# A two-layer decoder trunk on one core: the value pass with the coefficients standing in the array instead of the value rows

## The chip, the core and the metric

The kernel runs on one core of a Trainium2 chip. TensorE (PE) multiplies, VectorE (DVE), ScalarE (ACT) and GpSimd (POOL) do element work, SyncE (SP) issues most of the DMAs. A matrix product here has a stationary operand, which is loaded into the array (at most 128 columns), and a moving operand, which streams past it (at most 512 columns); the result is summed in a bank of PSUM, 128 partitions by 512 floats. There are eight banks. The metric is the device time of one execution in microseconds (us).

## The reference

Each of two layers mixes the 256 tokens (layer 0 an mLSTM, layer 1 an RG-LRU, both with cross-attention to a fixed memory), normalises, and then applies PEER, a mixture of 16,384 experts of which each token uses 8 x 16. The change is in the last two lines of PEER:

```python
u = u_tab[eid]
act = gelu(einsum('nhkd,nd->nhk', u, xb))
coef = (gw * act)
y = einsum('nhk,nhkd->nd', coef, v_tab[eid])
...
x = layer_norm(DN_ALPHA * x + y, ln2_g[i], ln2_b[i])
```

`v_tab` holds 16,384 rows of 1,024 floats. The kernel computes `y` for most tokens as a dense product over all experts, with a coefficient of zero where a token does not use one.

## The kernel before

**Tokens.** Of the 256 tokens the first N = 192 go the dense way. The last NS = 64 go row by row: `few` gathers each token's rows of `u` and `v` by indirect DMAs from POOL's queue (L1104) and sums them on DVE (L1124 for `u`, L1128 for `v`), 128 partitions by 1,024 elements an operation, 128 operations for `u` and 128 for `v` in a layer. `deal` (L1131) hands out these operations: each step of a pass adds a rate from RATES to a credit, and at 1.0 one operation is issued. At the step with `i + 2 == CLOSE` whatever is left is issued at once, and a DMA on SP's queue moves half of the sum to the other partitions.

**Values.** The dense coefficients of layer and pass lie in `wglo` and `wghi`: 128 blocks (one per group of 128 experts) of 128 partitions by 192 tokens. The value pass is the loop `for i in range(P)` in `peer_layer`: one step for each of the 128 groups. A step takes the group's 128 x 1,024 value rows from a ring of five raw buffers, filled by SP's DMAs. Since a product of float32 precision is made of three products of a shorter format, the rows are split: ACT casts them to the high part `wH` (L123), DVE subtracts for the low part `wL` (L138), in a ring of HL_BUFS = 3 pairs. The block of coefficients is split in the same way two steps ahead (`coef`: ACT L270, DVE L271) into a tile `cc`: 192 high columns and 192 low ones.

**Products.** In `products` the value rows stand and the coefficients move: for each of eight slices of 128 output columns, `wH` stands while the 384 columns of `cc` stream (L1373), then `wL` stands while the 192 high columns stream (L1374). The result is transposed: 128 output columns by 192 tokens, in eight banks, one for each slice.

**The end of a pass.** The last two groups (`kept`) are held back and multiplied slice by slice at the end, with three products of 192 columns each (L201 to L203). Then, for each slice, a product with the identity folds the high-by-low sums in (L1171), ACT copies the slice out (L1434), PE transposes it back to tokens in two parts (L1416 for tokens 0 to 127, the first tile; L1417 for tokens 128 to 191 of the second tile), and DVE adds it to `x` (L1422) and takes statistics (L1427). After the last slice `norm` forms mean and root for both tiles (L380 to L383), and scales: for part of the first tile ACT and POOL do it (`scale_beside`, L356 to L360), for the rest DVE (L344 and L349). In layer 1 the result is stored; that is the program's end. In layer 0 the rows are transposed for the next layer (`turn`, L370, then ACT L374 and DVE L375), and between these transposes PE works at six pieces of layer 1's memory keys and values (`memory`); then the RG-LRU layer begins with the query product over the new `x`, 24 products for the first four slices of `x` and 24 for the last four.

**Order.** All engines run their instructions in the order in which this code is written; nothing is rescheduled. An instruction waits for what it reads and for the buffers it writes.

## Time and profile before

| | us |
|---|---|
| median of three runs (1654.86 to 1657.91) | 1655.14 |
| the profiled execution | 1655.38 |
| its span, first to last instruction | 1653.6 |
| layer 0: first product of the value pass, first transpose for layer 1, first query product | 540.09, 845.65, 852.93 |
| layer 1: first product of the value pass, last transpose, end of the span | 1340.90, 1641.26, 1653.6 |

In the rows below, an engine's times are from the span's start. PE is one row per product or per run of products; "idle before" is the time in which the engine did nothing, with what ended it. Products are pipelined: the duration of one (0.36 us for 384 columns) is longer than the distance to the next, so the pace of a pass is read from the distance of starts. PEclk is the clock granted to TensorE, 1.00 being 2.4 GHz and 0.50 being 1.2 GHz.

### The profile page before, as it was taken

The page shows a single profiled execution, that of the slowest core. Times are in us where ns is not written, and L with a number is a line of the kernel's source. Part 1 is how long each engine was busy: PE and PEld are TensorE (multiplying, and loading weights), DVE is VectorE, ACT ScalarE, POOL GpSimd, SP SyncE. Part 2 cuts the span into 40 slices and gives each one's busy share as a digit, 9 for nine tenths or more (in the row PEclk, how much of TensorE's full clock was granted, in tenths as well). Part 3 has the DMA queues.
Part 4 walks back from the last instruction along what each step waited for, and adds up shares of the span by engine and source line. Part 5 has one row for each costly group of instructions (what it writes and reads, how often), then busy time and mean ns, then how long its engine had stood idle before and what let it go on. Part 6 is the DMA issues. An engine that isn't in the chain of part 4 may idle for free. (4 is left out here: it accounts for less than half of the span.)

```text
span 1653.6 us, 31410 instructions
## 1 busy us (share of the span) xinstructions
PE 1626.6 (98%) x11693; PEld 1607.6 (97%) x11693; DVE 1405.8 (85%) x2865; ACT 787.2 (48%) x1527; POOL 451.1 (27%) x362
## 2 busy tenths in 40 slices
PE   9999999999999999999999999999999999999996
PEld 9999999999999999999989899999999999999996
DVE  6676787899999898998878958888999988999976
ACT  6564334432226555555658442345222455555554
POOL 3004202432223333332100250133222333343301
PEclk9999999999999999999999999999999999999998
DMA  7655468988889999998856255799888999999973
GB/s 253 210 179 200 154 218 321 355 319 314 319 308 355 329 351 350 348 360 314 289 170 206 101 176 193 279 339 353 309 313 311 340 330 345 355 349 356 349 242 116
DMA packets 133784, 470.54 MB, mean 285 GB/s; under 512 B 14972, under 2 KB 18816, under 8 KB 133376
## 3 DMA queue, kind: packets, MB, share of 16 engines
q1 hardware_dynamic: 94984, 330.89, 57.4%
q0 software_dynamic: 36864, 134.23, 21.6%
q10 hardware_dynamic: 1784, 3.41, 0.6%
q8 instruction: 92, 1.51, 0.3%
q14 instruction: 60, 0.49, 0.1%
HBM read 465.46 MB, written 1.31 MB: 282 GB/s over the span
## 5 line engine op out<-in xcount | busy, mean ns | idle before, releaser
L138 DVE TENSOR_TENSOR wL<-raw,wH 128x1024 fp32r<-128x1024 f32 (+3 forms) x436 | 514.0, 1181 | 177.8 <-ACT wH L123 175.4
L123 ACT CAST wH<-raw 128x1024 fp32r<-128x1024 f32 (+2 forms) x445 | 456.1, 1027 | 390.2 <-PE bank L1373 235.5
L1373 PE MATMUL bank<-cc,wH 128*128 128x384 f32 x2016 | 575.6, 360 | 4.9 <-DVE cc L271 4.9
L1374 PE MATMUL bank<-cc,wL 128*128 128x192 f32 x2016 | 505.5, 251 | 1.9 <-DVE wL L138 1.9
L274 PE MATMUL bank<-xF,raw 128*128 128x192 f32 x2624 | 454.6, 328 | 0.0
L274 PEld LDWEIGHTS bank<-xF,raw 128*128 128x128 f32 x2624 | 423.0, 190 | 0.0
L1374 PEld LDWEIGHTS bank<-cc,wL 128*128 128x128 f32 x2016 | 386.5, 192 | 2.1 <-DVE wL L138 2.1
L1373 PEld LDWEIGHTS bank<-cc,wH 128*128 128x128 f32 x2016 | 379.5, 188 | 5.4 <-DVE cc L271 5.4
L1104 POOL DMA_INDIRECT row<-in_v_dram,lot x128 | 209.0, 1632 | 358.8 <-DVE rep L1128 315.6
L1104 POOL DMA_INDIRECT row<-in_u_rows_dram,lot x128 | 144.9, 1132 | 466.6 <-DVE wghi L1198 187.7
L1161 PE MATMUL bank<-xHL,wH 128*128 128x384 f32 x736 | 217.3, 360 | 0.0
L1162 PE MATMUL bank<-xHL,wL 128*128 128x192 f32 x736 | 184.5, 251 | 0.0
L1128 DVE SCALAR_TENSOR_TENSOR rep<-row,coefs,rep 128x1024 f32<-128x1024 f32 x124 | 158.4, 1278 | 0.1
L1124 DVE CUSTOM_DVE_ANT_0 row<-row,rep 128x1024 f32<-128x1024 f32 x128 | 155.7, 1217 | 0.0
L1162 PEld LDWEIGHTS bank<-xHL,wL 128*128 128x128 f32 x736 | 140.7, 191 | 0.0
L201 PE MATMUL bank<-xHL,wH 128*128 128x256 f32 x488 | 138.4, 284 | 0.0
L1161 PEld LDWEIGHTS bank<-xHL,wH 128*128 128x128 f32 x736 | 138.4, 188 | 0.0
L203 PE MATMUL bank<-xHL,wL 128*128 128x256 f32 x488 | 136.6, 280 | 0.1
L202 PE MATMUL bank<-xHL,wH 128*128 128x256 f32 x488 | 136.3, 279 | 0.0
L1195 ACT ACTIVATE wghi<-bank 128x192 f32<-128x192 f32 (+23 forms) x96 | 24.1, 252 | 206.9 <-PE bank L274 206.9
L202 PEld LDWEIGHTS bank<-xHL,wH 128*128 128x128 f32 x488 | 92.9, 190 | 0.3 <-DVE xHL L462 0.2
L203 PEld LDWEIGHTS bank<-xHL,wL 128*128 128x128 f32 x488 | 92.0, 189 | 0.4 <-DVE wL L138 0.3
(337 smaller groups left out, 1985.7 us busy)
## 6 DMA issues: line engine op xcount, KB each, us to landing
raw<-in_u_dram SPq DMA_DIRECT2D x256, 512.0 KB, 4.9
raw<-in_v_dram SPq DMA_DIRECT2D x256, 512.0 KB, 6.5
raw<-in_w_q_dram SPq DMA_DIRECT2D x32, 512.0 KB, 4.2
raw<-in_w_out_dram SPq DMA_DIRECT2D x16, 512.0 KB, 3.8
raw<-in_w0qx_dram SPq DMA_DIRECT2D x8, 512.0 KB, 5.1
raw<-in_w0v_dram SPq DMA_DIRECT2D x8, 384.0 KB, 5.0
raw<-in_w0o_dram SPq DMA_DIRECT2D x8, 384.0 KB, 2.9
raw<-in_w1x_dram SPq DMA_DIRECT2D x8, 384.0 KB, 3.0
```

The lines of the kernel that those rows point to most:

```text
L123: (nc.vector.tensor_copy if self.cast_dve else nc.scalar.copy)(h[:, c], r[:, c])
L138: rest = lambda l=l, r=r, h=h, c=slice(k, n): nc.vector.tensor_sub(l[:, c], r[:, c], h[:, c].bitcast(F32))
L202: mm(out, sH, mL, start=False, stop=False, skip_group_check=True)
L203: mm(out, sL, mH, start=False, stop=stop, skip_group_check=True)
L274: self.nc.tensor.matmul(out, lhsT, rhs, start=start, stop=stop, skip_group_check=True)
L1104: self.nc.gpsimd.indirect_dma_start(to, None, rows, bass.IndirectOffsetOnAxis(ap=self.lot[:, 0, n:n + 1].bitcast(I32), axis=0))
L1124: nc.vector.tensor_tensor_reduce(r, r, rep, 1.0, 0.0, ALU.mult, ALU.add, sums[:, n:n + 1])
L1128: nc.vector.scalar_tensor_tensor(acc[0] if n == NS - 1 else rep, r, c, rep, op0=ALU.mult, op1=ALU.add)
L1161: mm(two(g[:, :2 * N]), h[:, c], two(self.xHL[:, dt, :])[:, :, :N], start=dt == 0, stop=False, skip_group_check=True)
L1162: mm(g[:, :N], l[:, c], self.xH[:, dt, :N], start=False, stop=False, skip_group_check=True)
L1373: mm(y[s][:, :2 * N], h[:, c], cc[:, :2 * N], start=i_ == 0, stop=False, skip_group_check=True)
L1374: mm(y[s][:, :N], l[:, c], cc[:, :N], start=False, stop=False, skip_group_check=True)
```

## The change

The roles in the value pass are exchanged. Now 128 or 64 columns of coefficients stand, and 512 columns of value rows move. `cc` gets 64 more columns: [192 high | 192 low | the 64 high ones of tokens 128 to 191 again], the last by one more ACT copy. Columns 320 to 447 are then the low and the high coefficients of the 64 tokens of the second tile in one stationary tile, so that one product over `wH` gives low-by-high in partitions 0 to 63 and high-by-high in 64 to 127 (`second`, L1418); the high ones over `wL` (64 columns, L1416) are added to the lower half. The first tile takes three products (`first`, L1427, L1428, L1425). The result has tokens in partitions, as `x` has: four banks, no fold, no copy and no transpose back.

At the end of a pass the last HALVED groups (2 in layer 0, 6 in layer 1) are held back whole and the last KEPT (3 and 7) for half of the first tile. Their order is: the second tile, then the first tile's left half, then its right half in two quarters. For that layer 1 gets four more pairs of value buffers and seven more `cc` tiles, in the space of `wglo`, which is free from step 64 on, and looks further ahead from step 107 on (`lead`). `norm` has a new branch: ACT copies the upper half of the second tile's banks out, DVE adds both halves to `x`, and the second tile's statistics, root and scaling come between those of the first tile's quarters; POOL has no part in it. The dealing is spread: rate 0.55 to step 102 in layer 0, 0.505 to step 112 in layer 1, and the two additions of the gathered sums are cut in four, one in each of four steps.

```diff
-CLOSE, ADD = 104, 110
-RATES = (0.65, 0.85, 0.6, 0.52)
+CLOSES = (104, 114)
+RATES = (0.65, 0.85, 0.6, (0.55, 0.505))
+KEPT, HALVED = (3, 7), (2, 6)
...
             def coef(i):
-                cc = cp.tile([P, 512], F32R, name="cc")
-                self.split_to(cc[:, :N], cc[:, N:2 * N], block(i))
+                cc = ccs[i - P] if layer and i >= P - kept else cp.tile([P, 512], F32R, name="cc")
+                nc.scalar.copy(cc[:, :N], block(i))
+                nc.scalar.copy(cc[:, 2 * N:3 * N - P], block(i)[:, P:])
+                nc.vector.tensor_sub(cc[:, N:2 * N], block(i), cc[:, :N].bitcast(F32))
...
-            def products(s, part):
...
+            def second(part, k, low=False):
+                ks = slice(512 * k, 512 * k + 512)
                 for i_, (h, l), cc in part:
...
+                    if low:
+                        mm(y[2 + k][:N - P], cc[:, P:N], l[:, ks], start=False, stop=False, skip_group_check=True)
+                    else:
+                        mm(y[2 + k], cc[:, N + P:N + 2 * P], h[:, ks], start=i_ == 0, stop=False, skip_group_check=True)
+
+            def first(part, c0, n, low=False):
...
+                    if low:
+                        mm(out, cc[:, :P], l[:, cs_], start=False, stop=False, skip_group_check=True)
+                    else:
+                        mm(out, cc[:, :P], h[:, cs_], start=i_ == 0, stop=False, skip_group_check=True)
+                        mm(out, cc[:, N:N + P], h[:, cs_], start=False, stop=False, skip_group_check=True)
...
+                if i < P - HALVED[layer]:
+                    second(late[-1:], 0), second(late[-1:], 1)
+                    first(late[-1:], 0, 512)
+                    if i < P - kept:
+                        first(late[-1:], 512, 512)
+                        first(late[-1:], 512, 512, True)
+                    first(late[-1:], 0, 512, True)
+                    second(late[-1:], 0, True), second(late[-1:], 1, True)
...
+            end = late[-HALVED[layer]:]
+            for k in range(2):
+                second(end, k), second(end, k, True)
+            first(end, 0, 512), first(end, 0, 512, True)
+            for c0 in (512, 768):
+                first(late, c0, 256), first(late, c0, 256, True)
```

The end of `norm`'s new branch, the part for layer 1 (`piece` adds a quarter of the first tile to `x` and takes its statistics; `scale` is `center` and `spread`):

```diff
+            aggr(1, 2)
+            nc.vector.scalar_tensor_tensor(x[:, 0, half0], x[:, 0, half0], alpha, y[0], op0=ALU.mult, op1=ALU.add)
+            for q in range(2):
+                nc.vector.bn_stats(st[:, 0, q, :], x[:, 0, q * Q:(q + 1) * Q])
+            root(1)
             if last:
...
                 scale(1, 0, 2), store(nc.scalar, 1, 0, 2)
+                piece(2)
+                scale(1, 2, 2), store(nc.sync, 1, 2, 2)
+                piece(3)
+                aggr(0, 4)
+                root(0)
+                scale(0, 0, 2), store(nc.scalar, 0, 0, 2)
+                center(0, 2, 2)
                 for q in (2, 3):
+                    spread(0, q, 1), store(nc.sync, 0, q, 1)
                 return
```

In layer 0 the new branch scales and transposes quarter by quarter, second tile first, and leaves the last halves of both tiles to be transposed between the two halves of the query product.

PE's order in a step of layer 0's value pass. Before, a slice takes two products; names stand as out<-in, without saying which operand stands, and the shape is out's partitions by moving columns. The first three of eight slices:

```order
L1373 MATMUL bank_5861<-cc_5829,wH_5795 128x384
L1374 MATMUL bank_5861<-cc_5829,wL_5796 128x192
L1373 MATMUL bank_5862<-cc_5829,wH_5795 128x384
L1374 MATMUL bank_5862<-cc_5829,wL_5796 128x192
L1373 MATMUL bank_5863<-cc_5829,wH_5795 128x384
L1374 MATMUL bank_5863<-cc_5829,wL_5796 128x192
```

The same step of the changed kernel, whole:

```order
L1418 MATMUL bank_5865<-wH_5795,cc_5829 128x512
L1418 MATMUL bank_5866<-wH_5795,cc_5829 128x512
L1427 MATMUL bank_5863<-wH_5795,cc_5829 128x512
L1428 MATMUL bank_5863<-wH_5795,cc_5829 128x512
L1427 MATMUL bank_5864<-wH_5795,cc_5829 128x512
L1428 MATMUL bank_5864<-wH_5795,cc_5829 128x512
L1425 MATMUL bank_5864<-wL_5796,cc_5829 128x512
L1425 MATMUL bank_5863<-wL_5796,cc_5829 128x512
L1416 MATMUL bank_5865<-wL_5796,cc_5829 64x512
L1416 MATMUL bank_5866<-wL_5796,cc_5829 64x512
```

Sixteen products over 4,608 columns became ten over 5,120, and `wH` is read by the first six alone.

DVE's order where the dealing ends in layer 1's value pass (`rep` and `wghi` are the gathered sums, `wL` the low part of value rows, `cc` that of coefficients). Before:

```order
L1128 SCALAR_TENSOR_TENSOR rep_10481<-row0_10482,coefs_10488,rep_10481 128x1024
L138 TENSOR_TENSOR wL_17362<-raw_17234,wH_17361 128x1024
L1128 SCALAR_TENSOR_TENSOR rep_10481<-row1_10483,coefs_10488,rep_10481 128x1024
L1128 SCALAR_TENSOR_TENSOR rep_10481<-row2_10484,coefs_10488,rep_10481 128x1024
L1128 SCALAR_TENSOR_TENSOR wghi_12747<-row3_10485,coefs_10488,rep_10481 128x1024
L271 TENSOR_TENSOR cc_17373<-wghi_12747,cc_17373 128x192
L138 TENSOR_TENSOR wL_17393<-raw_17261,wH_17392 128x1024
```

In the changed kernel, where its last operation of `few` stands (`vL` are the added buffers):

```order
L1169 SCALAR_TENSOR_TENSOR rep_9781<-row2_9784,coefs_9788,rep_9781 128x1024
L146 TENSOR_TENSOR wL_16316<-raw_16235,wH_16315 128x1024
L1401 TENSOR_TENSOR cc_16321<-wghi_12051,cc_16321 128x192
L146 TENSOR_TENSOR vL3_15368<-raw_16255,vH3_15367 128x1024
L146 TENSOR_TENSOR vL0_15362<-raw_16274,vH0_15361 128x1024
L1401 TENSOR_TENSOR cc_16343<-wghi_12051,cc_16343 128x192
L1169 SCALAR_TENSOR_TENSOR wghi_12051<-row3_9785,coefs_9788,rep_9781 128x1024
L146 TENSOR_TENSOR wL_16359<-raw_16280,wH_16358 128x1024
```

Three operations of `few` in a row, ahead of a `cc`, are gone; steps with two splits of value rows have come in.

DVE's last rows of the program. Before, from the last two slices on:

```order
L1422 SCALAR_TENSOR_TENSOR x_76<-x_76,bank_18063 128x128
L1422 SCALAR_TENSOR_TENSOR x_76<-x_76,bank_18063 64x128
L1427 BN_STATS st_17963<-x_76 128x6 x2
L380 BN_AGGR mv_18074<-st_17963 128x2 x2
L382 RECIPROCAL rs_18075<-rs_18075 128x2
L383 SCALAR_TENSOR_TENSOR nm_18076<-mv_18074,rs_18075 128x2
L344 SCALAR_TENSOR_TENSOR x_76<-x_76,mv_18074,raw_17848 128x512
L349 SCALAR_TENSOR_TENSOR x_76<-x_76,rs_18075,raw_17873 128x512
```

In the changed kernel, from the third quarter of the first tile on:

```order
L392 SCALAR_TENSOR_TENSOR x_76<-x_76,bank_14006 128x256
L393 BN_STATS st_16581<-x_76 128x6
L352 SCALAR_TENSOR_TENSOR x_76<-x_76,mv_16666,raw_16486 128x512
L357 SCALAR_TENSOR_TENSOR x_76<-x_76,rs_16667,raw_16507 128x512
L392 SCALAR_TENSOR_TENSOR x_76<-x_76,bank_14006 128x256
L393 BN_STATS st_16581<-x_76 128x6
L396 BN_AGGR mv_16666<-st_16581 128x2
L347 RECIPROCAL rs_16667<-rs_16667 128x1
L352 SCALAR_TENSOR_TENSOR x_76<-x_76,mv_16666,raw_16486 128x512
L357 SCALAR_TENSOR_TENSOR x_76<-x_76,rs_16667,raw_16507 128x512
```

The second tile's scaling (L352 and L357 between the two L392) stands ahead of the last quarter's addition; behind the last quarter only the first tile's is left.

## Rows read from the trace of the kernel before

**Rows 1.** The page's head and engine line: busy time, share of the span and number of instructions.

```profile
span 1653.6 us, 31410 instructions
PE 1626.6 (98%) x11693; PEld 1607.6 (97%) x11693; DVE 1405.8 (85%) x2865; ACT 787.2 (48%) x1527; POOL 451.1 (27%) x362
```

**Rows 2.** Stretches of the span: from:to, length, then busy time (and instructions) of PE, PEld, DVE, ACT and POOL, granted clock, DMA share and GB/s. The first is in layer 0's value pass, the second just ahead of it, the third behind the end of layer 1's dealing.

```profile
600.00:660.00 60.00, 60.00 (x423) 60.00 (x423) 54.40 (x67) 34.54 (x54) 22.28 (x14) 1.00 0.97 354
500.00:540.00 40.00, 40.00 (x287) 39.94 (x286) 36.78 (x53) 23.54 (x53) 17.04 (x11) 1.00 0.98 364
1580.40:1583.80 3.40, 3.36 (x13) 3.36 (x13) 2.79 (x4) 0.00 (x0) 0.00 (x0) 0.50 0.71 178
```

**Rows 3.** PE in order of time (start, duration), two products of layer 1's value pass, 72 pairs of L1373 and L1374 apart (nine steps).

```profile
1400.07 0.36 PE L1373 MATMUL bank<-cc,wH 128*128 128x384 f32 x1
...
1420.55 0.36 PE L1373 MATMUL bank<-cc,wH 128*128 128x384 f32 x1
```

**Rows 4.** PE in order of time in layer 0's output projection, products of 512 moving columns: six distances from the first row to the second, thirteen from there to the third.

```profile
118.71 0.39 PE L201 MATMUL bank<-eH,mixH 128*128 128x512 f32 x1
...
120.10 0.39 PE L201 MATMUL bank<-eH,mixH 128*128 128x512 f32 x1
...
123.05 0.39 PE L202 MATMUL bank<-wL,mixH 128*128 128x512 f32 x1
```

**Rows 5.** Groups of instructions by line and shape: count, busy time, mean ns of one, idle time before them with what ended it.

```profile
L138 DVE TENSOR_TENSOR wL<-raw,wH 128x1024 fp32r<-128x1024 f32 x372 | 455.1, 1225 | 123.5 <-ACT wH L123 121.5
L1128 DVE SCALAR_TENSOR_TENSOR rep<-row,coefs,rep 128x1024 f32<-128x1024 f32 x124 | 158.4, 1278 | 0.1
L271 DVE TENSOR_TENSOR cc<-wghi,cc 128x192 fp32r<-128x192 f32 x128 | 47.8, 374 | 0.2
L270 ACT CAST cc<-wghi 128x192 fp32r<-128x192 f32 x128 | 44.5, 347 | 7.8 <-PE bank L1374 7.8
```

**Rows 6.** PE in order of time where it waited in the value passes (layer 0 twice, layer 1 once), and the seventh product of L1373 behind layer 1's wait; in brackets the idle time and what ended it.

```profile
779.10 0.44 PE L1373 MATMUL bank<-cc,wH 128*128 128x384 f32 x1 [2.19 <-DVE cc L271]
799.62 0.36 PE L1374 MATMUL bank<-cc,wL 128*128 128x192 f32 x1 [1.87 <-DVE wL L138]
1580.44 0.69 PE L1373 MATMUL bank<-cc,wH 128*128 128x384 f32 x1 [2.72 <-DVE cc L271]
1583.75 0.41 PE L1373 MATMUL bank<-cc,wH 128*128 128x384 f32 x1
```

**Rows 7.** DVE in order of time ahead of two of these waits.

```profile
794.73 1.22 DVE L1401 SCALAR_TENSOR_TENSOR x<-x,wghi 64x1024 f32<-64x1024 f32 x1
795.99 1.22 DVE L1402 TENSOR_TENSOR x<-x,wghi 64x1024 f32<-64x1024 f32 x1
...
1575.67 2.60 DVE L1128 SCALAR_TENSOR_TENSOR rep<-row,coefs,rep 128x1024 f32<-128x1024 f32 x2
1578.83 1.28 DVE L1128 SCALAR_TENSOR_TENSOR wghi<-row,coefs,rep 128x1024 f32<-128x1024 f32 x1 [0.57 <-DMA row<-in_v_dram,lot]
```

**Rows 8.** PE in order of time in layer 1: the first product of the value pass, the first of the held-back groups, the last slice's transpose.

```profile
1340.90 0.36 PE L1373 MATMUL bank<-cc,wH 128*128 128x384 f32 x1
...
1632.19 0.28 PE L201 MATMUL bank<-cc,wH 128*128 128x192 f32 x1
...
1641.13 0.30 PE L1416 MATMUL bank<-ident,wghi 128*128 128x128 f32 x1 [0.99 <-DVE x L1422]
```

**Rows 9.** DVE in order of time at the program's end.

```profile
1642.64 0.37 DVE L380 BATCH_NORM_AGGREGATE mv<-st 128x2 f32<-128x24 f32 x2
1643.37 0.17 DVE L382 RECIPROCAL rs<-rs 128x2 f32<-128x2 f32 x1 [0.36 <-ACT rs L381]
...
1643.65 0.74 DVE L344 SCALAR_TENSOR_TENSOR x<-x,mv,raw 128x512 f32<-128x512 f32 x1
...
1645.10 1.21 DVE L344 SCALAR_TENSOR_TENSOR x<-x,mv,raw 128x512 f32<-128x512 f32 x1
...
1648.61 1.22 DVE L349 SCALAR_TENSOR_TENSOR x<-x,rs,raw 128x256 f32<-128x256 f32 x2
```

**Rows 10.** POOL in order of time there: its first operation beside DVE.

```profile
1644.66 1.10 POOL L359 TENSOR_TENSOR x<-x,raw 128x256 f32<-128x256 f32 x1 [72.64 <-ACT x L356]
```

**Rows 11.** PE in order of time at the end of layer 0: the first product of the value pass, the first product of the memory's pieces, two more of them 33 distances apart (256 columns each), two transposes with waits, the first query product.

```profile
540.09 0.36 PE L1373 MATMUL bank<-cc,wH 128*128 128x384 f32 x1
...
840.76 0.36 PE L201 MATMUL bank<-memH,kH 128*128 128x256 f32 x1
...
841.08 0.28 PE L203 MATMUL bank<-memH,kL 128*128 128x256 f32 x1
...
844.96 0.28 PE L203 MATMUL bank<-memH,kL 128*128 128x256 f32 x1
845.65 0.66 PE L370 MATMUL bank<-ident,x 128*128 128x128 f32 x4 [0.41 <-DVE x L349]
...
850.66 0.66 PE L370 MATMUL bank<-ident,x 128*128 128x128 f32 x4 [1.11 <-DVE x L349]
...
852.93 0.37 PE L201 MATMUL bank<-xHL,wH 128*128 128x256 f32 x1
```

**Rows 12.** DVE and ACT in order of time there: DVE's addition and statistics of two quarters, and ACT's copy of the finished query product.

```profile
834.46 0.74 DVE L1422 SCALAR_TENSOR_TENSOR x<-x,bank 128x256 f32<-128x256 f32 x2 [2.66 <-PE bank L1417]
835.13 0.74 DVE L1427 BATCH_NORM_STATS2 st<-x 128x6 f32<-128x256 f32 x2
...
859.24 0.59 ACT L840 COPY xqT<-bank 128x512 f32<-128x512 f32 x1 [2.34 <-PE bank L203]
```

More of the change, by code (lines that the diff above doesn't have):

```diff
@@ L52, in plain, with extra_of @@
     return i < 16 or i < 50 and i % 2 or N0 <= i < N0 + STEPS or i == P - 1
+def extra_of(layer, i):
+    n = KEPT[layer]
+    k = i - (P - 3 * n)
+    return k % n // 2 if layer and k >= 0 and k % n % 2 == 0 else None
 MEM1 = (109, 111, 113, 115, 117, 119, 121)
@@ L390, in norm @@
                 for q in (2, 3):
-                    spread(1, q, 1), store(nc.sync, 1, q, 1)
+                    spread(0, q, 1), store(nc.sync, 0, q, 1)
                 return
-            scale_beside(1, 1)
-            scale(1, 0, 1), scale(0, 0, 1)
+            piece(2)
+            scale(1, 0, 1)
+            piece(3)
+            aggr(0, 4)
             scale(1, 1, 1)
+            root(0)
+            scale(0, 0, 1)
+            next(fill), next(fill)
+            turn(1, 0, 1)
+            next(fill)
@@ L1220, in peer_layer @@
             coefs = sp.tile([P, NS], F32, name="coefs")
+            lo_p = right.enter_context(ExitStack())
+            lo = lo_p.enter_context(tc.tile_pool(name=f"lo{layer}", bufs=1, side="right")).tile([P, N0, N], F32, name="wglo")
             flat = lambda t, b: t[:, b:b + 6, :].rearrange("p a b -> p (a b)")[:, :D]
@@ new lines, in lead @@
+            def lead(i):
+                return min(HL_BUFS + max(0, min(kept - HL_BUFS, (i - RISE) // 3)), P - i)
+            for i in range(P):
+                late.append((i, self.next(lead(i)), cs.pop(0)))
+                if layer and i == N0:
+                    lo_p.close()
+                    t = right.enter_context(tc.tile_pool(name="tail1", bufs=1, side="right"))
+                    self.extra = [[t.tile([P, D], F32R, name=f"v{z}{c}") for z in "HL"] for c in range(kept - HL_BUFS)]
+                    ccs += [t.tile([P, 512], F32R, name=f"cc{c}") for c in range(kept)]
+                    t.tile([P, 8], F32, name="gap")
+                if i + 2 == CLOSES[layer]:
@@ L1396, in peer_layer @@
                 if i > 1:
-                    self.deal(few, RATES[3])
-                if i == ADD:
-                    rs = slice(P - NS, P)
-                    xs = self.x[rs, 1]
-                    nc.vector.scalar_tensor_tensor(xs, xs, ALPHA, last[0][rs], op0=ALU.mult, op1=ALU.add)
-                    nc.vector.tensor_add(xs, xs, last[1][rs])
-                if i + 1 > P - kept:
-                    continue
-                for s in range(DT):
-                    products(s, list(late))
@@ L1407, in peer_layer @@
-                late = []
+                    self.deal(few, RATES[3][layer])
+                if 0 <= i - CLOSES[layer] - 2 < 4:
+                    z, k = divmod(i - CLOSES[layer] - 2, 2)
+                    rs, ks = slice(P - NS, P), slice(512 * k, 512 * k + 512)
+                    xs = x[rs, 1, ks]
+                    nc.vector.scalar_tensor_tensor(xs, xs, 1.0 if z else ALPHA, last[z][rs, ks], op0=ALU.mult, op1=ALU.add)
+                if i < P - HALVED[layer]:
[6 more added lines that the diff above has]
+                    second(late[-1:], 0, True), second(late[-1:], 1, True)
+                    if i < P - kept:
+                        late.pop()
@@ L1431, in peer_layer @@
-            for s in range(DT):
-                products(s, late)
-                self.fold(y[s], self.xHL[:, s])
-                nc.scalar.copy(hi[:, s, :], y[s][:, :N])
-                if s == 1:
-                    turn(0)
-                elif s == 2:
-                    turn(1), onto(0), count(0)
-                elif s > 2:
-                    turn(s - 1)
-                if s in (4, 6):
-                    onto(s // 2 - 1), count(s // 2 - 1)
-            onto(3, 0, P)
-            turn(DT - 1), onto(3, P, P), count(3)
+            end = late[-HALVED[layer]:]
@@ L1460, in memory @@
                     yield self.mem_v(self.vb, (2 * c + 2, 2 * c + 3), KV[1], *self.kvw[c], 4)
-            for _ in self.norm(None, False, False, memory()):
+            for _ in self.norm(y, False, False, memory()):
                 pass
@@ L1500, in tail @@
             for i in range(P):
-                self.add(A["v"][layer, i], D)
+                self.add(A["v"][layer, i], D, extra_of(layer, i))
                 if layer == 0 and i in MEM1:
```

85 lines of the change are left out of this document (37 added, 48 removed).

## The prediction

> **What bounds the kernel now.** I read the page's engine line first: PE is busy 98% of the span [rows 1], so time can only come from fewer or shorter products, or from PE's waits. Then the stretches: in a value pass PE is busy throughout, DVE 54.40 of 60 us (91%), ACT 34.54 us, and the DMA engines hold a share of 0.97 at 354 GB/s, against 0.98 at 364 GB/s just ahead of it [rows 2]. So PE sets the pace, with DVE and the DMAs close behind: whatever makes a step much shorter than now runs into them, and whatever makes it longer costs its full price. Then PE's own rows for the pace, its few waits, and the two ends of the passes, where PE is not the bound and a chain over DVE is.
>
> **The pace of a step.** Before: 72 pairs in 20.48 us [rows 3], 0.2844 us a pair, eight pairs a step: 2.276 us. Now: ten products of 512 columns. The trace has such products with another operand standing: 13 distances in 2.95 us, 0.227 each, once they run; six in 1.39 us, 0.232 each, just behind a wait [rows 4]. Ten make 2.27 or 2.32 us. I take 0.228 (eight of ten at the first, two at the second, since a step's first products still check semaphores): 2.280 us. So the step is worth nothing, 0.004 us x 128, although it streams 11% more columns: sixteen loads of weights became ten. Bounds: 0.227 throughout gives -2.6 us over the 2,560 products of both layers, 0.232 gives +10 us. I let the range reach somewhat less high than this, since the value pass streams for hundreds of us and the slow distances in the trace lie behind waits.
>
> What the Trainium skill says here is different: "TensorE: Matmul & The Clock Gate", section "Back-to-back issue gap", gives columns / 2.4 + 2.5 ns, 216 ns for 512 columns. The row has 227, so the trace does not agree; by the page the step would be an estimated 2.16 us.
>
> **Other engines in a step.** ACT gets one more copy of 128x64 a group; a copy of 128x192 takes 0.347 us [rows 5], so it costs between 0 and 0.35 us, and ACT is idle 42% of a step [rows 2]: hidden. DVE's work is unchanged, 1.225 for values, 0.374 for coefficients, 1.278 for a dealt row [rows 5]; busy time says 2.06 us a step (0.907 x 2.276). Rate 0.55 instead of 0.52 adds 0.04: 2.10 of 2.28, no bound. In DMA terms a step moves 0.524 MB of values and 0.55 of that by gathers, 0.813 MB in 2.28 us: 356 GB/s, below the 364 seen. Layer 1's 0.505 is lighter. `wH` is free after six of ten products instead of at a step's end, so ACT's casts start 0.9 us earlier: slack, no gain by itself.
>
> **PE's waits inside the passes.** Layer 0 waited 2.19 us for `cc` and 1.87 us for `wL`, layer 1 2.72 us for `cc` [rows 6]. Each lies behind a burst on DVE: the last operations of `few` (three in a row, 2.60 + 1.28 us with a wait for a gather), and the two additions of 1.22 us each [rows 7]. The order of the changed kernel has no such burst: a dealt row stands between splits to the end, and the additions are quartered. I cost them at nothing (an operation of 64x512 is half of 1.22 us, a step has 0.2 us to spare and a coefficient two steps ahead). Behind layer 1's wait the clock was granted at 0.50 for 3.4 us [rows 2], and six pairs took 3.31 us [rows 6] instead of 1.71: 1.6 us more that go with the wait.
> What may be late instead: from step 107 to 112 of layer 1 two or three additional splits of 1.2 us meet the dealing, some 1.8 us of backlog on DVE against a lead of about 1.6 to 2.5 us; and the last coefficient of the held-back six is formed behind the last cast. I put 0.5 us on it; bounds 0 and 2.7 (the old wait again).
>
> **The end of layer 1.** Products from 1340.90 [rows 8]: 128 steps x 2.280 = 291.8; splitting 21 products of 512 columns into 42 of 256 at 0.1176 (33 distances in 3.88 us [rows 11]) adds 0.13; 0.5 for the lateness: the last product is over at E = 1633.3. Before, the held-back groups only began at 1632.19 and the last transpose came at 1641.13 [rows 8]. Of the tail the second tile's part is done before E: behind its last product lie (6 x 3 x 0.228) + 42 x 0.1176 = 9.0 us of products, and its DVE work up to the scaling is about 5.5 us, its scaling 4 x 0.75 = 3 us more. Behind E: DVE ends that scaling (0.4), adds the last quarter and takes its statistics (0.4 + 0.4, half of the 0.74 of [rows 12]), aggregates, root and reciprocal: 1.0 (from 1642.64 to 1643.65 [rows 9]), then four more operations of 512 columns, 0.74 each while POOL is silent: 3.1 with their gaps. (With POOL beside it DVE took 1.21 for the same shape [rows 9, 10]; the new branch has nothing on POOL.) That is E + 5.3 = 1638.6. DVE's last operation ended at 1648.61 + 1.22 = 1649.83, and the stores behind it took 3.8 us to the end of the span [rows 1, 9]; they are as large now: 1642.4, 11.2 us earlier than 1653.6. Bounds for this chain: everything beside the last quarter hidden or 2 us of it not, -12.5 to -9.
>
> **The end of layer 0.** Products from 540.09 [rows 11], 291.8 + 0.05: E = 832.0. Before, the memory's products began at 840.76 [rows 11]. But here DVE sets the end. The second tile's last product is at E - 3.5; from there DVE works off both halves of the second tile (2 x 2.1 us: additions, copy, statistics), half the first tile (1.5), then by quarters 0.75 + 0.9 + 0.75 + 0.2 + 0.9 + 0.15 + 0.9: the first tile's first quarter is scaled at E + 6.6. One transpose, copy and subtraction later comes the next quarter (E + 8.65), its low parts E + 9.75, a split of weights E + 10.95, four scalings of 512 columns E + 13.95. PE meanwhile has six memory pieces of 1.41 and waits about 2.6 us between them; it starts the query product at E + 11.9, its first 24 products end at E + 14.7, eight transposes at E + 15.65, and the last halves of the new `x` are ready at E + 17.2; 24 more products end at E + 20.0 = 852.0. Before, they ended at 859.2 [rows 12]. So of the 8.8 us that PE is earlier, 7.2 arrive. Bounds: -8.8 (all of it) to -4 (if the DVE operations of 64 partitions and the extra ACT hop cost 3 us more than I have from [rows 12]).
>
> **Sum.** -11.2 - 7.2 = -18.4 us, the pace included. From the profiled execution's 1655.38 that is 1637.0; it lies 0.24 above the median of the runs, 1655.14, which the rounding to 1637 covers.
>
> **The rivals.**
> A. The products of 512 columns keep the slower distance of 0.232 in the value pass: 2,560 x 0.004 = +10 us, 1647. For it: six of the nineteen distances in [rows 4] are of this kind, and each step has semaphores to check. Against: they fall to 0.227 within seven products, and PE's queue stays full in the pass. 12%.
> B. The other side: the same mechanism further up. A standing tile of 64 columns and two tiles in turns over four banks are not in the trace; if a product then takes over 0.235, all that the ends bring is gone (2,560 x 0.0072 = 18.4 us); at 0.238 the kernel ends at 1663. For it only that the shape is unseen; against, all 512-column rows that do not stand behind a wait. 4%.
> C. One end is hidden anyway: in layer 0 the RG-LRU layer may wait for weights or for DVE instead of taking the 7.2 us (DVE's splits follow its scaling in the same queue). 1644. For it: DVE is the engine that sets this end. Against: all of PE's idle time is 27 us [rows 1], and the waits and ends treated here hold some 22 of it, so little is left for waits of that layer. 8%.
> D. The change does not do what it says: the second tile is finished first on PE, but its DVE work is late and stands behind E after all, about 7 us in layer 1: 1644 to 1645. Against: 9.0 us of products cover 8.5 us of DVE work. 4%.
> E. The products follow each other so closely that the DMAs set the step: 0.797 MB (0.524 x 1.52) at the 364 GB/s of [rows 2] are 2.19 us, 256 x 0.09 = 23 us less than forecast, 1614. That wants less than 0.219 us a product; [rows 4] never show it, and [rows 3] lie 0.044 above columns / 2.4 for a pair (576 columns, 0.240). 2%. The page's gap of 216 ns named above is what would bring it there.
> The forecast itself: 70%, between 1632 and 1643.
>
> **Range and chances.** From 1630 (pace at 0.227, all of layer 0's 8.8 us, no lateness: 1637 - 2.6 - 1.6 - 0.5 = 1632, and a little) to 1648 (rival A, with C and D below it). About 0.2% or 3.3 us is what a measurement can tell from no change: faster than 1651.8 in 92% (the forecast, A, C, D, E less their bad corners), within it 4%, slower 4% (B's upper part and a DVE or DMA shortage that I don't see).
>
> **What would show it.** In the new profile: distances of 0.227 to 0.23 between the products of a step; no PE wait above 1 us in either pass and no stretch at clock 0.50 ahead of the end; the last product about 1633 minus layer 0's gain (1626), DVE's last operation 5 us behind it and the span's end 3.8 us behind that; the query product of layer 0 over at about 852. Wrong would be: PE waiting for `cc` around steps 107 to 115 of layer 1, a DMA share at 1 with waits for raw buffers in layer 0, or distances above 0.232.

## The result, and the profile after

The changed kernel takes 1647.65 us (median of four runs, 1645.83 to 1647.97), the kernel before, beside it on the same chip, 1656.43 (1654.86 to 1657.91): a ratio of 0.9945, 95% interval 0.9928 to 0.9962. That is 8.8 us or 0.5% faster, where 18.4 us were forecast; the time lies at the upper edge of the range. The profiled execution took 1647.97 us. The page's head and engine line, against [rows 1]:

```profile
span 1646.2 us, 28666 instructions
PE 1625.4 (99%) x10107; PEld 1471.5 (89%) x10107; DVE 1408.0 (86%) x2863; ACT 818.4 (50%) x1755; POOL 442.9 (27%) x356
```

PE has 1586 products fewer and is busy just as long; only its weight loads are 136 us shorter. So the page alone says that the exchange of roles bought no time on PE, and the gain must lie in waits and at the ends of the passes. The span splits at five starts of products, the same in both traces (value pass: first and last product with `cc` as an operand):

| us | before | forecast | after |
|---|---|---|---|
| layer 0's value pass, first to last product | 298.63 | 291.8 | 294.63 |
| from there to the first query product | 14.21 | 12.0 | 12.43 |
| from there to layer 1's value pass | 487.97 | 489.8 | 492.69 |
| layer 1's value pass, first to last product | 298.63 | 292.3 | 296.06 |
| from there to the end of the span | 14.09 | 9.2 | 10.57 |

What stands ahead of the first row moved by 0.3 us, without meaning: in the runs of this study the first pass begins anywhere from 539.1 to 540.9 us. (The third row is longer than before by design: eight transposes and half of the scaling now lie behind the first query product.) The misses against the forecast are 2.8, 0.4, 2.9, 3.8 and 1.4 us, 11.3 in all, and lie in three places.

**The pace.** PE in order of time in layer 1, from the pair of narrow products over `wL` (64 standing columns) into the next step, and the same pair nine steps on; it answers to [rows 3]:

```profile
1401.20 0.63 PE L1416 MATMUL bank<-wL,cc 128*64 128x512 f32 x2
1401.66 0.62 PE L1418 MATMUL bank<-wH,cc 128*128 128x512 f32 x2
1402.12 0.40 PE L1427 MATMUL bank<-wH,cc 128*128 128x512 f32 x1
1402.36 0.39 PE L1428 MATMUL bank<-wH,cc 128*128 128x512 f32 x1
1402.58 0.40 PE L1427 MATMUL bank<-wH,cc 128*128 128x512 f32 x1
1402.82 0.39 PE L1428 MATMUL bank<-wH,cc 128*128 128x512 f32 x1
...
1421.90 0.63 PE L1416 MATMUL bank<-wL,cc 128*64 128x512 f32 x2
```

20.70 us for nine steps: 2.300 a step, 0.230 a product, not 0.228. In both layers it is the same within 2 ns, step by step, and so are the ten distances in a step, each from a product's start to the next one's, read from the records: `second` over `wH` 224 and 231 ns, the first tile's four products over `wH` 236, 228, 233, 231, its two over `wL` 226 and 226, `second` over `wL` (the narrow ones) 236 and 229. Only the two products just ahead of the narrow ones run at the settled 226 to 227 ns of [rows 4].

**The end of layer 0.** PE, then DVE, then ACT in order of time, the place of [rows 11, 12], and a window's line (from:to, length, busy time of PE, PEld, DVE, ACT and POOL, granted clock, DMA share, GB/s):

```profile
849.58 1.03 PE L378 MATMUL bank<-ident,x 128*128 128x128 f32 x8
851.34 0.38 PE L209 MATMUL bank<-xHL,wH 128*128 128x256 f32 x1 [0.72 <-ACT xHL L382]
853.31 0.58 PE L210 MATMUL bank<-xHL,wH 128*128 128x256 f32 x1 [1.58 <-DVE xHL L383]
853.69 0.42 PE L211 MATMUL bank<-xHL,wL 128*128 128x256 f32 x1
...
856.46 0.29 PE L209 MATMUL bank<-xHL,wH 128*128 128x256 f32 x1
```

```profile
849.11 0.69 DVE L100 COPY kmT<-bank 64x512 f32<-64x512 f32 x1
849.84 2.10 DVE L146 TENSOR_TENSOR wL<-raw,wH 128x1024 fp32r<-128x1024 f32 x2
851.96 1.29 DVE L383 TENSOR_TENSOR xHL<-bank,xHL 128x512 fp32r<-128x512 f32 x2
```

```profile
850.22 1.07 ACT L382 CAST xHL<-bank 128x512 fp32r<-128x512 f32 x2 [3.47 <-PE bank L378]
...
857.71 0.59 ACT L881 COPY xqT<-bank 128x512 f32<-128x512 f32 x1 [5.68 <-PE bank L211]
```

```profile
853.00:857.00 4.00, 3.69 (x19) 3.69 (x20) 1.78 (x4) 0.00 (x0) 0.00 (x0) 0.57 0.77 249
```

The first query product is 6.1 us earlier than before, the finished query (ACT's copy) only 1.5 us. Behind the transposes PE waits 0.72 us for ACT's high parts, and then 1.58 for DVE's low parts, whose subtractions stand behind a copy and two splits of weights in DVE's queue (one of 128x1024 and one of 128x768, merged in the row). From 853.7 to 856.46 the products are 0.21 us apart instead of 0.115, at a granted clock of 0.50; the window's mean of 0.57 is made of both levels.

**The end of layer 1.** The only wait in the pass, PE at the first product of a held-back group, then PE's last product, then DVE in order of time, the place of [rows 8, 9]:

```profile
1621.10 0.47 PE L1418 MATMUL bank<-vH,cc 128*128 128x512 f32 x1 [0.93 <-DVE cc L1401]
```

```profile
1635.61 0.28 PE L1425 MATMUL bank<-vL,cc 128*128 128x256 f32 x1
```

```profile
1630.89 0.69 DVE L407 SCALAR_TENSOR_TENSOR x<-x,bank 128x512 f32<-128x512 f32 x1 [1.10 <-PE bank L1425]
...
1635.92 0.42 DVE L392 SCALAR_TENSOR_TENSOR x<-x,bank 128x256 f32<-128x256 f32 x1 [2.05 <-PE bank L1425]
1636.38 0.43 DVE L393 BATCH_NORM_STATS2 st<-x 128x6 f32<-128x256 f32 x1
1636.72 0.73 DVE L352 SCALAR_TENSOR_TENSOR x<-x,mv,raw 128x512 f32<-128x512 f32 x1
1637.49 0.75 DVE L357 SCALAR_TENSOR_TENSOR x<-x,rs,raw 128x512 f32<-128x512 f32 x1
1638.16 0.41 DVE L392 SCALAR_TENSOR_TENSOR x<-x,bank 128x256 f32<-128x256 f32 x1
...
1641.99 0.88 DVE L357 SCALAR_TENSOR_TENSOR x<-x,rs,raw 128x256 f32<-128x256 f32 x2
```

DVE idles 2.05 us ahead of the third quarter's addition (the row at 1635.92), which starts only behind the very last product, though the quarter's own products were over 2.5 us before (21 products at 0.12 us follow them). Both right quarters lie in one bank, and by the records only the last of the bank's 42 products raises the semaphore that the addition waits for. The left half, in another bank, was added from 1630.89 on, when PE had begun (at 1630.69) to write the right half's bank. And the scaling of the second tile's right half, which could have filled that idle time, stands behind it in the queue.

### The profile page after: what moved, and what is told of

It is laid out like the page before. It is cut to its first block, busy times and chain, and to the rows that moved or that the text cites. A ratio compares the mean times of both kernels' runs of the same rounds, so it can differ in the third digit from the quotient of the medians.

```text
span 1646.2 us, 28666 instructions
## 1 busy us (share of the span) xinstructions
PE 1625.4 (99%) x10107; PEld 1471.5 (89%) x10107; DVE 1408.0 (86%) x2863; ACT 818.4 (50%) x1755; POOL 442.9 (27%) x356
## 5 line engine op out<-in xcount | busy, mean ns | idle before, releaser
L146 DVE TENSOR_TENSOR wL<-raw,wH 128x1024 fp32r<-128x1024 f32 (+3 forms) x424 | 500.1, 1181 | 164.0 <-ACT wH L131 161.8
L131 ACT CAST wH<-raw 128x1024 fp32r<-128x1024 f32 (+2 forms) x433 | 443.7, 1026 | 322.9 <-PE bank L1428 175.2
L1427 PE MATMUL bank<-wH,cc 128*128 128x512 f32 (+1 forms) x494 | 194.1, 393 | 0.0
L1428 PE MATMUL bank<-wH,cc 128*128 128x512 f32 (+1 forms) x494 | 191.7, 388 | 0.0
L1416 PE MATMUL bank<-wL,cc 128*64 128x512 f32 x488 | 153.2, 394 | 0.0
L1418 PE MATMUL bank<-wH,cc 128*128 128x512 f32 x488 | 151.6, 391 | 0.1
L1425 PE MATMUL bank<-wL,cc 128*128 128x512 f32 (+1 forms) x494 | 151.0, 386 | 0.0
L1203 PEld LDWEIGHTS bank<-xHL,wL 128*128 128x128 f32 x736 | 140.6, 191 | 0.0
L1202 PEld LDWEIGHTS bank<-xHL,wH 128*128 128x128 f32 x736 | 138.4, 188 | 0.0
L1418 PEld LDWEIGHTS bank<-wH,cc 128*128 128x128 f32 x488 | 91.3, 187 | 35.2 <-ACT cc L1399 0.5
```

Source lines behind the costliest of these rows:

```text
L131: (nc.vector.tensor_copy if self.cast_dve else nc.scalar.copy)(h[:, c], r[:, c])
L146: rest = lambda l=l, r=r, h=h, c=slice(k, n): nc.vector.tensor_sub(l[:, c], r[:, c], h[:, c].bitcast(F32))
L1202: mm(two(g[:, :2 * N]), h[:, c], two(self.xHL[:, dt, :])[:, :, :N], start=dt == 0, stop=False, skip_group_check=True)
L1203: mm(g[:, :N], l[:, c], self.xH[:, dt, :N], start=False, stop=False, skip_group_check=True)
L1416: mm(y[2 + k][:N - P], cc[:, P:N], l[:, ks], start=False, stop=False, skip_group_check=True)
L1418: mm(y[2 + k], cc[:, N + P:N + 2 * P], h[:, ks], start=i_ == 0, stop=False, skip_group_check=True)
```

## The experiments

All are edits of the changed kernel. Where a time between two starts is given, it is one of the table above, from the run's trace, beside the changed kernel's. The median of the kernel before lay between 1656.2 and 1657.6 us beside these runs (1659.0, a single run, beside e9), so a difference of a microsecond between two medians shows little, and the intervals of e2, e3, e4, e6 and e7 overlap that of the changed kernel. The stretches are steadier: in the five runs that leave the way from the first query product to layer 1's value pass alone (e1, e2, e4, e5, e9) it takes 492.64 to 492.85 us, and the end behind the last product 10.55 to 10.57 us in the six that leave that alone.

**e1_wide: the narrow products made wide.** The products over `wL` get the 128 standing columns of the products over `wH`; for the 64 tokens this adds the product of low by low parts, which the kernel leaves out otherwise.

```diff
-mm(y[2 + k][:N - P], cc[:, P:N], l[:, ks], start=False, stop=False, skip_group_check=True)
+mm(y[2 + k], cc[:, N + P:N + 2 * P], l[:, ks], start=False, stop=False, skip_group_check=True)
```

> The products of value rows' low parts for the second tile take the same 128 standing columns as those of the high parts, instead of 64 (the upper half of the bank then also gets the low-by-high products and the lower half the small low-by-low ones, which the sum of the halves may hold). Theory 1: the changed kernel's step takes 2.300 us instead of 2.267 because each change between loads of 64 and of 128 columns disturbs the next seven or eight products; then every distance becomes 0.227, the step 2.267, and the kernel 2 x 128 x 0.033 = 8.4 us faster than the changed one (about 1639). Theory 2: the disturbance comes from the two semaphore waits of a step; then the step stays at 2.29 to 2.30 and the time at 1647. Theory 3: a standing tile of 128 columns costs a longer load than one of 64; then the step gets longer than 2.300.

Measured: 1640.18 us (1637.92 to 1641.45), ratio to the kernel before 0.9891 (0.9875 to 0.9908): 7.5 us less than the changed kernel's median. Nine steps in its trace:

```profile
1401.99 0.61 PE L1416 MATMUL bank<-wL,cc 128*128 128x512 f32 x2
...
1422.39 0.61 PE L1416 MATMUL bank<-wL,cc 128*128 128x512 f32 x2
```

20.40 us, 2.267 a step: every product now stands 226 or 227 ns behind the one ahead. The semaphores are those of the changed kernel, so they are not the cause. The value passes get 4.1 and 3.6 us shorter (290.51, 292.48). Wider loads of weights, which take longer themselves (188 ns against 134 or 135 by the records), made the pass faster.

**e5_one_wide: one of the two made wide.** The same edit for the second of the pair alone.

> Of the two products with the values' low parts in a step, the second has the 128 standing columns of the products with the high parts, the first keeps its 64 columns. Theory 1 (a change between loads of 64 and of 128 columns disturbs the products behind it, however many narrow ones there are): the step falls little from 2.300 us, to 2.285 or more, since one narrow load a step is left and the seven or eight products behind it still run at 226 to 236 ns. Theory 2 (each narrow load costs its own product some 16 ns): half of the 0.033 us by which all-wide loads shorten the step comes back, 2.283 us, with only two distances above 229 ns in a step. Theory 3 (it is the sum of narrow output partitions, not the load): as theory 2. The single distances tell it: many at 229 to 236 ns for theory 1, two for theory 2.

Measured: a single run, 1645.66 us. Nine steps:

```profile
1400.43 0.40 PE L1419 MATMUL bank<-wL,cc 128*64 128x512 f32 x1
1400.67 0.39 PE L1417 MATMUL bank<-wL,cc 128*128 128x512 f32 x1
...
1421.01 0.40 PE L1419 MATMUL bank<-wL,cc 128*64 128x512 f32 x1
```

20.58 us, 2.287 a step: 0.020 of the 0.033 us stay with one narrow load. The records give 236 ns behind the narrow one, then 228, 233 and 231, then 226 or 227. So a single narrow load disturbs the distance behind its own product and three more, not two distances (theories 2 and 3) and not seven or eight as theory 1 had it; with a pair of them it is eight. Nor does each narrow product cost something: in the held-back groups of layer 1 six of them stand in a row, and where they follow products at the settled pace, as in the changed kernel from 1625.23 us on, the distances are 236, 229, 224, 227, 234 and 231 ns and then 227 again. That is 21 ns more than six at 226.7, as much as the single one costs here. A product with 64 standing columns also writes only 64 partitions, so the load and the output change together, and what in the array makes the products behind pay is not shown.

**e2_old_dealing: the dealing as before.** Rate 0.52, closing at step 102 (`CLOSES` 104) in both layers, the two additions whole at step 110. (A layer has 64 operations of `few` for `u` and 64 for `v`; 128 each is the number over both layers.)

```diff
-CLOSES = (104, 114)
-RATES = (0.65, 0.85, 0.6, (0.55, 0.505))
+CLOSES = (104, 104)
+RATES = (0.65, 0.85, 0.6, (0.52, 0.52))
...
-                if 0 <= i - CLOSES[layer] - 2 < 4:
...
+                if i == 110:
```

> The changed kernel with the old dealing: rate 0.52 in both layers, the rest of the gathered rows at step 102 at once, both additions at once at step 110. Theory of the prediction: PE's three waits come back (about 2.2 and 1.9 us in layer 0, 2.7 us in layer 1 and 1.6 us of half clock behind it), so the kernel is 7 to 9 us slower than the changed one, 1655 to 1656: the dealing alone carries all that the change has brought. Rival: the new order frees the high parts after six of ten products, so the buffers are further ahead and hide half of the burst; then it is 3 to 4 us slower, and the rest of the gain has come from the ends.

Measured: 1650.85 us (1650.18 to 1656.41), ratio 0.9969 (0.9951 to 0.9986): 3.2 us more. The passes get 2.9 and 0.6 us longer (297.48, 296.63). PE's longest waits in the two passes:

```profile
779.95 0.70 PE L1418 MATMUL bank<-wH,cc 128*128 128x512 f32 x2 [1.39 <-DVE cc L1401]
...
813.36 0.73 PE L1418 MATMUL bank<-wH,cc 128*128 128x512 f32 x2 [0.48 <-ACT wH L131]
...
1582.82 0.70 PE L1418 MATMUL bank<-wH,cc 128*128 128x512 f32 x2 [1.55 <-ACT vH L131]
```

The waits are back, but smaller than in [rows 6]: 1.39 and 0.26 us for `cc`, 0.48 and 1.55 for ACT's high parts, 3.7 us in all against 6.8 and no half clock behind them. In layer 1 the wait of 0.93 us at the held-back groups is gone in return. So the other dealing is worth some 3 us; the rest of the old waits went with the rest of the change (the new roles and layer 1's added buffers), which no run here takes apart.

**e3_fill: PE kept busy at layer 0's end.** Twenty transposes of the identity, which compute nothing, behind the eight late transposes.

```diff
                 turn(1, 2, 2), turn(0, 2, 2)
+                self.idle(20)
```

> Twenty transposes of the identity (2.2 us) are put on PE in layer 0 where it waits for the last halves of the new x before the second half of the query product. Theory: PE's idle 2.7 us there let the clock fall to 0.50 for 3.4 us; with PE busy it stays at 1.00, the products that ran at 0.213 us run at 0.117, and the query product is over about 1.5 us earlier, 1646. Rival: the wait is set by DVE and the clock falls elsewhere or the transposes themselves delay the products; then the time does not move or is up to 1 us longer.

Measured: 1646.5 us (1645.97 to 1647.71), ratio 0.9933 (0.9917 to 0.995). The clock is granted at 1.00 from 846 to 862 us:

```profile
853.00:857.00 4.00, 3.62 (x31) 3.42 (x30) 2.60 (x5) 0.00 (x0) 0.00 (x0) 1.00 0.81 242
```

The product that waits for DVE's low parts starts 6.46 us behind the first query product, as in the changed kernel, so the filling neither delays nor hastens it. From the first query product to layer 1's value pass it takes 491.48 instead of 492.69 us: 1.2 us came back with the clock.

**e6_split_behind: the split of weights behind the subtractions.** In the query's loop of the RG-LRU layer the first call looks two tiles ahead instead of three, which moves one split of 128x768 behind the low parts.

```diff
-                h, l = self.next()
+                h, l = self.next(2 + c)
```

> At the start of the layer behind layer 0's value pass the split of the second pair of weights that is not needed yet (128x768) stands on DVE behind the two subtractions of the last halves' low parts instead of ahead of them. Theory (that queue on DVE is what PE waits for there): the wait of 1.6 to 1.85 us before the 25th query product falls by 1.0 us, the end comes 1.0 us earlier than in the changed kernel, 1645.2 in a profile, and up to 1.6 us more if the clock then stays at 1.00 behind it. Rival (the wait comes from ACT's copies of the high parts, and DVE's queue is hidden): no change, 1646.2, the wait stays.

Measured: 1645.0 us (1644.92 to 1645.12), ratio 0.9933 (0.9917 to 0.995), 2.65 us less. PE's row and DVE's:

```profile
851.25 0.38 PE L209 MATMUL bank<-xHL,wH 128*128 128x256 f32 x1 [0.73 <-ACT xHL L382]
852.34 0.38 PE L210 MATMUL bank<-xHL,wH 128*128 128x256 f32 x1 [0.71 <-DVE xHL L383]
```

```profile
849.74 1.23 DVE L146 TENSOR_TENSOR wL<-raw,wH 128x1024 fp32r<-128x1024 f32 x1
851.00 1.29 DVE L383 TENSOR_TENSOR xHL<-bank,xHL 128x512 fp32r<-128x512 f32 x2
```

```profile
853.00:857.00 4.00, 4.00 (x38) 4.00 (x36) 2.06 (x5) 1.73 (x3) 0.00 (x0) 1.00 0.73 249
```

The wait for DVE fell by 0.87 us, and the clock stayed at 1.00: from the first query product to layer 1's value pass 490.09 us, 2.6 less and 0.3 from the forecast. So the split in the queue was the cause of 0.87 us of the wait and of the half clock. The half clock is absent in all four runs with this edit (e6, e7, e8, e10); the changed kernel and all five runs with neither this edit nor the filling have it at this place.

**e7_behind_fill: both.** As e6, with eight transposes of the identity (e3 has twenty).

> As the run before, and 8 transposes of the identity (they compute nothing) on PE behind the eight transposes of the last halves. Theory (half clock and DVE's queue add up): the clock is granted at 1.00 from 846 to 862 us, the layer-1 value pass begins 2.3 to 2.7 us earlier relative to the first query product than in the changed kernel (492.7 us between them there, 490.2 here), 1643.7 in a profile. Rival (only one of the two counts, or layer work behind it waits for something else): 491.5 us between them, as in the run with 20 transposes alone, 1645.

Measured: 1645.93 us (1645.71 to 1648.81), ratio 0.9944 (0.9928 to 0.9961); 490.45 us there, so the filling gives nothing once the split has moved. Layer 1's pass was 0.9 us longer than in e6, at the waits ahead of the held-back groups, which vary from run to run.

**e4_last_order: layer 1's end in another order.** The held-back groups' coefficients are formed from step 114 on, one more a step, and the second tile's right half is scaled ahead of the first tile's third quarter.

```diff
-                    cs.append(coef(i + 2))
+                    cs.append(pre.pop(i + 2) if i + 2 in pre else coef(i + 2))
+                if layer and P - 2 * kept <= i < P - kept:
+                    pre[i + kept] = coef(i + kept)
...
-                piece(2)
                 scale(1, 2, 2), store(nc.sync, 1, 2, 2)
+                piece(2)
```

> Layer 1's end in another order: the coefficients of the seven kept groups are split seven steps ahead, one a step, and DVE scales the second tile's right half before it adds the first tile's third quarter. Theory: PE's wait of 1.2 us (and 0.3 in slow products behind it) at the first held-back product goes, and 1.5 us of scaling move from behind the last product into a wait of 2.05 us on DVE: 2.5 to 3 us faster, 1645. Rival: the third quarter's addition waits for the bank's last product whatever stands ahead of it (that stays so in both), and the added splits delay others; then 1.4 us or less.

Measured: 1645.18 us (1644.56 to 1646.66), ratio 0.9928 (0.9911 to 0.9944), 2.5 us less. DVE at the same place:

```profile
1633.34 0.75 DVE L357 SCALAR_TENSOR_TENSOR x<-x,rs,raw 128x512 f32<-128x512 f32 x1
1634.69 0.42 DVE L392 SCALAR_TENSOR_TENSOR x<-x,bank 128x256 f32<-128x256 f32 x1 [0.60 <-PE bank L1425]
```

The last product starts at 1634.37 here; the scaling is done before it ends, and the quarter still waits for it. From that product to the end it takes 9.12 us instead of 10.57, and the pass 0.7 us less (295.37): the wait of 0.93 us is gone, and a shorter one for `cc`, 0.33 us at 1610.92, has come in.

**e9_no_quarters: the right half whole.** On e4, the held-back groups' right half as one product of 512 columns.

```diff
-            for c0 in (512, 768):
-                first(late, c0, 256), first(late, c0, 256, True)
+            first(late, 512, 512), first(late, 512, 512, True)
```

> On the run with the other order of the end: the second half of the first tile in the held-back groups is again one product of 512 columns instead of two of 256. Theory (both quarters lie in one bank, DVE may not add the third before the last product of the bank is over, so the cut brings nothing): from the last product's start to the end of the span it stays within 0.3 us of the 9.12 us that the run with the other order has, and the products themselves get 0.2 us shorter; both ends together a gain of 0 to 0.5 us. Rival (the third quarter's addition does go ahead of the last product): 0.8 us longer, the third quarter's addition and statistics.

Measured: a single run, 1645.03 us. From the last product's start to the end 9.22 us against 9.12. The third quarter's addition starts as before right behind the last product:

```profile
1634.47 0.42 DVE L392 SCALAR_TENSOR_TENSOR x<-x,bank 128x256 f32<-128x256 f32 x1 [0.34 <-PE bank L1425]
```

So the cut into quarters brings nothing as the kernel has it, with both in one bank; quarters in two banks were not tried. (The pass itself was 1.2 us shorter than in e4, 294.17 us, with no wait left at the held-back groups; in layer 0, where there is none in either run, pass and way to the query product together take 307.06 us in both.)

**e8_all and e10_best: what gained, together.** e8 has the edits of e1, e4 and e7; e10 those of e1, e4, e6 and e9.

> All that gained alone: 128 standing columns in the products with the low parts, the held-back coefficients formed one a step and the second tile's scaling ahead of the first tile's third quarter, the split behind the subtractions, and the 8 filling transposes. If the gains add: 7.5 us from the standing columns, 2.5 from the order of the end, 2.5 from layer 0's end, 12.5 us off 1647.65: 1635. Rival (they share a wait, DVE's work at the two ends): 1638 or more.

> The run with all gains, without its 8 filling transposes and with the held-back first-tile products whole instead of quartered. Theory: the filling cost 0.36 us where the split already stands behind the subtractions (490.45 against 490.09 us from the first query product to layer 1's value pass), the quarters cost 0.2 us a layer: 0.8 us less than 1635.41, 1634.6. Rival (behind the query another wait takes what comes earlier, as the 0.7 us wait at 1118 us of the run with all gains did): no change, 1635.4.

Measured: e8 1635.41 us (1634.84 to 1635.8), ratio to the kernel before 0.9875 (0.9858 to 0.9891); e10 1635.10 us (1634.47 to 1635.75), 0.9872 (0.9855 to 0.9888). Both beat the changed kernel by 12 us, and the gains add. Between the two the runs tell nothing. In e8's trace 1.2 us of what comes early is lost between the query and layer 1's value pass (491.67 us against e7's 490.45), where PE has a wait of 0.66 us at 1114.76 us; in e10's trace that wait isn't there and the way takes 490.26 us, so the loss belongs to that execution rather than to the edits, as far as one trace of each can say. e8's value passes take 290.54 and 290.90 us.

## Why the prediction was right and wrong

**Right.** The direction, and part of what gives it: PE's waits at the closing of the dealing are gone in both passes (one of 0.93 us is left in layer 1, at the held-back groups), no half clock there, and the first query product comes 0.4 us from where the steps put it. ACT's additional copies cost nothing (50% busy; where PE waits in a pass, at 1621.10, DVE's part of `cc` is the last to be ready), and DVE and the DMAs set no step: with the same work for both, e1 has a step of 2.267 us. What was not right in it is the share of the dealing: I let all 8.4 us of waits and clock go with the bursts; undoing the dealing alone brings 3.2 back.

**Wrong: the pace, 5.1 us of the 11.3.** The step that failed is "eight of ten at the first, two at the second". It is the other way round: eight of the ten distances are off the settled pace (224 to 236 ns) and two on it, 0.230 us in the mean instead of 0.228; three of the ten lie above 0.232, a sign of being wrong that the prediction had named. The slower distances of [rows 4] were read as something that a wait leaves behind it. Read one by one from the records, in that trace of the kernel before, with 128 standing columns in every product, they are, behind three distances of 342, 383 and 339 ns, 231, 231, 236, 228, 233 and 230 ns, and then 227. That is the sequence in the new step (231, 236, 228, 233, 231, 226). So the same return to the pace follows a hold-up and a narrow load; in [rows 4] it comes once, in the new step the narrow loads start it over each time. The bounds 0.227 and 0.232 held, and the miss is half of rival A's. That rival gave semaphores as a reason, which e1 rules out; rival B had the right suspicion, the unseen shape of 64 columns, and priced it at 18 us or more.

The Trainium skill ("TensorE: Matmul & The Clock Gate", section "Back-to-back issue gap") gives the 216 ns of the prediction for an isolated product, and some 131 ns as the sustained distance at 512 columns in a stream of loads and products. No run here agrees: with equal loads it settles at 226.7 ns.

**Wrong: the end of layer 0, 2.9 us.** The step that failed is "the last halves of the new `x` are ready at E + 17.2; 24 more products end at E + 20.0" (E is the end of the pass's last product). I counted DVE's work for `x` and left out what else is issued to DVE there: one split more than the query needs. The low parts were done at 853.25, E + 18.7, and the half clock behind the two waits took another 1.2 us (e3). Rival C had named that queue ("DVE's splits follow its scaling in the same queue") at 8%, and as hiding the whole gain of 7.2 us; e6 gives 2.6 us back by moving one instruction. (The terms up to the first scaled quarter add up to E + 6.75, not E + 6.6: an error of 0.15 us in the sum.)

**Wrong: layer 1, 1.2 us in the pass and 1.4 behind it.** The lateness of 0.5 us came to 1.7 us (the pass misses by 1.2 beyond the pace): the 0.93 us wait and slow products around it; the bounds 0 to 2.7 held. Behind E, the step that failed is "ends that scaling (0.4), adds the last quarter": it assumed that three of the four quarters would be done by then. They were not, since DVE waits for the last product of the bank that holds both right quarters. So a quarter and its statistics (0.8 us) and 1.0 us of scaling more than forecast lie behind E, and the stores behind DVE's last operation gave 0.5 us of that back (3.3 us instead of 3.8). e4 moves the scaling ahead and gets 1.45 us back. The Trainium skill bears on this wait in "PSUM — Partial Sum Buffer", section "PSUM bank collisions raise a hardware error": two engines are to be kept apart by bank and by quadrant of 32 partitions, not by address. The row at 1635.92 agrees in that the program keeps them so; no run here tries an earlier addition.

**The chances.** I set A and C beside the forecast as if one alone could happen. Half of A (5.1 of 10 us) and 2.9 of C's 7.2 us came together, with 2.6 us at the end of layer 1, and the sum lay at the upper edge of the range.

## What to carry to other kernels

Where products and weight loads alternate for hundreds of us, keep all loads the same width, even if a wider one computes something superfluous. Read the distances of one whole step, not one settled run of another shape. At a hand-over between stages list everything that stands in the queue of the engine that sets it, weights for later stages too, and move what is not needed yet; a wait that leaves PE idle can cost more than its length through the clock (1.2 us on top of 2.3 here). Cutting a result finer brought nothing here while the pieces lay in one bank and the reader waited for the bank's last product.

## What the runs showed of the hardware

- A load of 64 columns between loads of 128 makes its product and the ones behind it slower: 236, 228, 233, 231 ns against 226.7 with equal loads (e5); a pair of them puts eight of ten off the pace (mean of the ten 230), and six in a row cost 21 ns in all. The same sequence follows a hold-up where all loads have 128 columns (231, 236, 228, 233, 230 in [rows 4]).
- Waits of 0.72 and 1.58 us with one product between them were followed by some 3 us at the half clock; waits of 0.73 and 0.71 at the same place (e6) were not.
- PE's loads became 136 us shorter in all and PE's busy time stayed at 1625 us; with 26 us more of load time (e1: 1497.9) the kernel was 7.5 us faster. Load time that is hidden behind the products told nothing of the pace here.
